# Order of work in a hybrid decoder layer: first group's routing and decoding first, then the second group's natural projections

## The chip, the cores and the metric

The kernel runs on one core of one Trainium2 chip. Its metric is the device time of one execution in microseconds (us). Three runs of the kernel before took 2902.53 to 2905.03 us, with a median of 2904.23 us. Five engines work side by side: TensorE (PE: matmuls; PEld is its loading of weights), VectorE (DVE), ScalarE (ACT), GpSimd (POOL) and SyncE (SP), the last two mostly issuing transfers.

## The reference, cut to what matters

One decoder layer over 1024 tokens of width 1024, all in float32. A normalized input goes through retention (4 heads) and differential attention (4 heads), both are projected out and added to the input; then comes a feed-forward part of 16384 single-neuron experts:

```python
h = rmsnorm(x, norm_mix_g); proj = h @ w_in              # rq rk rv rg dq dk dv
x = x + concat(silu(rg) * rmsnorm(retention(rq, rk, rv)), diff_out(dq, dk, dv)) @ w_out
xb = rmsnorm(x, norm_ffn_g)
q = (xb @ wq).reshape(t, 8, 2, 128)                      # 8 heads, two halves
s = einsum('thpd,hpkd->thpk', q, subkeys)                # 128 keys a half
s_top, i_top = top_k(s, 16)                              # of each half
c_top, c_idx = top_k(all 256 sums of two halves, 16)
e = i1 * 128 + i2; g = softmax(c_top)                    # 128 experts a token
act = gelu(einsum('thkd,td->thk', u[e], xb))
x = x + einsum('thk,thkd->td', g * act, v[e]); return rmsnorm(x, final_norm_g)
```

## The kernel before, in words

The 1024 tokens are eight tiles of 128. The first three tiles are the first group (`gs` in the code, tiles 0 to 2, "sparse"), the last five the second (`gd`, tiles 3 to 7, "dense"). Both go through `front`, a generator that emits the steps of a group: normalization and transposing (`split_t`, L197), two natural projections (`proj_n`, L176: token rows out, weights `wn`, four chunks each; up to the mark "projected"; the second one is evacuated through `dvt` tiles and written to HBM at L234 to L237), head projections (`proj_t`), retention and attention by head (up to "mixed"), a third natural projection, the output projection (L403, up to "summed"), a second normalization with transposing (L411 to L427, up to "routing"), and routing (L433 to L470): for each of 16 query blocks 24 projection matmuls (`psT`), a copy by ScalarE, the scores (`psc`, L445), and top-16 searches on VectorE; every second block also searches the sums.

All matmuls on weights take a float32 operand as two parts: a chunk of weights is loaded (`wraw`, four buffers), ScalarE makes the high part (L152, tag `uh`) and VectorE the low part (L154, `wlo`, tag `ul`), two buffers of each, and three matmuls are made of each product (L159 to L161).

The feed-forward part is done in two ways. For the first group the chosen rows of `u` and `v` are gathered: 3 tiles x 128 choices, one indirect DMA of 512 KB by GpSimd and one VectorE instruction for each row of `u` (L860, L862) and of `v` (L867, L869), 768 gathered rows in all; here a gathered row means one such step of 128 tokens. Before that, `sparse_routes` (L529) decodes the choices of each tile into indices (`decode`, L482, one-hot comparisons L505 to L514; indices at L537). For the second group all 128 x 128 experts are computed densely on TensorE (`psH`, `psHs` for inputs, `kp`, `psV` for outputs), with a gate matrix `g_d` built in between (`dense_routes`, `build_g`).

The gathered rows, the decoding tiles and several others of the early stages (among them `dvt`) share one group of five buffers, `ug`. At the end of the program `xt` and the running sum of a tile of gathered rows take the places (`sx`, `sa`) of the first group's routing results, which decoding reads.

Order is set in two ways. The order of the program text is the priority by which a planner, which works with a simulated timeline at build time, fixes the order of instructions on each engine; `weave(a, b, na, nb)` (L650) interleaves two generators at na steps to nb. The gathered rows come last in the text, so they have the lowest priority and go into VectorE's free places. They are held back by `gated` (L673): each step that passes through it adds `per` permissions, and the n-th gathered instruction is planned no sooner than the VectorE instruction that was the last one when the n-th permission was given. After the last such permission all others come free with the first dense expert (L807).

Around the change the order before is: the first group up to "summed", woven with the second group's first normalization; the second group's two natural projections (8 steps) woven 8 to 19 with the first group's second normalization and routing; then the second group from its head projections to "routing" (80 steps), woven 6 to 1 with `sparse_routes` (3 steps), at 1.5 permissions a step; then dense routing with spilled experts, gate matrices, and the dense experts.

Of the kernel before, what the change touches and what calls it, by code (L numbers as in the profile page):

```python
# [48 lines left out]
RAW = 4  # L49
UG = 5  # L50
BIGS = 4
ROUTE = 6
MIX = 3
ACTS = 1
AHEAD = 1
SPILL = 39
PACE = (8, 3)
SLOW = 4
PER = (1.5, 1.5, 0.0)
NC2 = 80  # L60
TC = {"schedule_with_timeline_sim": True}

# [36 lines left out]
def layer_kernel(ctx, tc, x, wt, wn, wo, wq, sk, ut, u, v, gmix, gffn, gfin, gsub, dlam, consts, alb, out):  # L99
# [418 lines left out]
    def gates_of(rp, late, nt, tag):  # L518

        cv = late.cv.rearrange("p t h k -> p (t h) k")  # L520
        mz = rp.tile([P, 2, nt * PH], F32, tag=tag[0], bufs=tag[1], name="mz")
        V.tensor_copy(mz[:, 0], cv[:, :, 0])
        V.tensor_sub(cv, cv, mz[:, 0, :, None].to_broadcast([P, nt * PH, K]))
        A.activation(cv, cv, AF.Exp)
        V.tensor_reduce(mz[:, 1], cv, axis=AX.X, op=ALU.add)
        V.reciprocal(mz[:, 1], mz[:, 1])
        V.tensor_mul(cv, cv, mz[:, 1, :, None].to_broadcast([P, nt * PH, K]))

    def sparse_routes(rp, late, g0, nt, *rooms):  # L529

        gates_of(rp, late, nt, rooms[0])
        for lt in range(nt):
            t = ST.index(g0 + lt)
            V.tensor_copy(gA[t].rearrange("p (h k) -> p h k", h=PH), late.cv[:, lt])
            i1, i2 = decode(rp, late, lt, *rooms)
            V.scalar_tensor_tensor(i1, i1, float(NK), i2, op0=ALU.mult, op1=ALU.add)
            V.tensor_copy(idxA[t].rearrange("p (h k) -> p h k", h=PH), i1)  # L537
            yield

    def dense_routes(rp, gp, pp, late):  # L540

        before = None
        gates_of(rp, late, ND, ("mz", 1))
        for t in range(ND):
            i1, i2 = decode(rp, late, t)
            ps = pp.tile([P, 4, P], F32, tag="B", bufs=2, name="psR")
            for c, src in enumerate((i2, i1, late.cv[:, t])):
                PE.transpose(ps[:, c], src.rearrange("p h k -> p (h k)"), ident)
            r = rp.tile([P, P // 8, 4, 8], F16, tag="rt", bufs=2, name="rt")
            by = ps.rearrange("p c (q t) -> p q c t", t=8)  # L550
            A.activation(r[:, :, 0:2], by[:, :, 0:2], AF.Copy)
            A.activation(r[:, :, 2], by[:, :, 2], AF.Copy, scale=GS)
            V.scalar_tensor_tensor(r[:, :, 3], by[:, :, 2], GS, r[:, :, 2], op0=ALU.mult, op1=ALU.subtract)
            lo = rp.tile([P, P // 8, 8], F32, tag="rl", bufs=2, name="rl")
            if ACTS:
                A.activation(lo, r[:, :, 3], AF.Copy)
            if before is not None:
                yield from build_g(gp, pp, *before)
            else:
                yield  # L560
            before = r, lo, t
        yield from build_g(gp, pp, *before)
# [84 lines left out]
    def pool(name, es=ctx, **kw):  # L647
        return es.enter_context(tc.tile_pool(name=name, bufs=1, reuse_waits="tile", **kw))

    def weave(a, b, na=1, nb=1):  # L650

        i = j = 0
        while a is not None or b is not None:
            if b is None or (a is not None and i * nb <= j * na):
                i += 1
                try:
                    yield next(a)
                except StopIteration:
                    a = None
            else:  # L660
                j += 1
                try:
                    yield next(b)
                except StopIteration:
                    b = None
# [3 lines left out]
    def last_dve():  # L669
        ins = nc.cur_bb.bb.instructions  # L670
        return next(i for i in reversed(ins) if i.engine == V.engine).name

    def gated(g, per):  # L673

        due = 0.0
        for y in g:
            due += per[y == "turned"]
            while due >= 1.0:
                gates.append(last_dve())
                due -= 1.0  # L680
            yield y

    def run(g):
        for _ in g:
            pass

    def until(g, mark):
        for y in g:
            if y == mark:
                return  # L690
            yield y

    sp = pool("sp")
# [34 lines left out]
    def spills(pf):  # L728
        for i, ei in enumerate(early):
            two = pf.tile([P, 2, 512], F32, tag="A", bufs=2, name="psHs")  # L730
            SY.dma_start(hs_d[i], experts_in(ei, lambda hf: two[:, hf]))
            yield

    with ExitStack() as es:
        pf = pool("pf", es, space=bass.MemoryType.PSUM)
        ms, md = SimpleNamespace(), SimpleNamespace()
        with ExitStack() as e2:
            fs = pool("fs", e2)
            ms.tp = ms.vp = ms.fp = ms.hp = ms.np = md.tp = fs
            md.hp, md.np, md.vp = wp, wp, lp  # L740
            ug = ("ug", UG)
            ms.big = md.big = (sp, *ug)
            lates = Routed(sp, sn, ("sx", "sa"))
            gs = front(ms, pf, cst, s0, sn, False, lates)
            gd = front(md, pf, cst, d0, dn, True, late)
            with ExitStack() as e3:
                ms.ap = pool("fa", e3)
                run(until(gs, "normed"))
                front_consts(cst, cp, wp)
                run(until(gs, "mixed"))  # L750
            run(weave(until(gs, "summed"), until(gd, "normed"), 15, 5))
            run(weave(until(gd, "projected"), gs, 8, 19))
        with ExitStack() as e2:
            fd = pool("fd", e2)
            md.tp = md.ap = md.fp = fd
            md.big = (fd, "big", BIGS)
            run(gated(weave(until(gd, "routing"), sparse_routes(sp, lates, s0, sn, ug, ug, ug), ROUTE, 1), PER[:2]))
            gh = spills(pf)
            run(weave(gd, islice(gh, 16 // SLOW), SLOW, 1))
        gp = pool("gp", es)  # L760
        run(gated(weave(dense_routes(gp, gp, pf, late), gh, *PACE), (PER[2], 0)))

# [89 lines left out]
    for t in range(NS):  # L852
# [5 lines left out]
        for k in range(HK):  # L858
            ug = sp.tile([P, D], F32, tag="ug", bufs=UG, name="ug")
# [49 lines left out]
```

## Time and profile before

| | before |
|---|---|
| runs | 2902.53 to 2905.03 us, median 2904.23 |
| profiled execution | 2900.81 us, span 2899.0 us |
| mean granted TensorE clock | 0.975 |
| PE busy | 2712.1 us (94%), 16043 matmuls |
| DVE busy | 2363.5 us (82%) |
| ACT busy | 1063.9 us (37%) |
| POOL busy | 1047.4 us (36%) |
| DMA | 741.34 MB, mean 256 GB/s |

The span runs from the first to the last instruction of the profiled execution; 1.8 us of its time lie outside. Matmuls are pipelined: one takes some 0.3 to 0.4 us in the records, while the next starts 0.14 to 0.23 us after it, so pitches are read from starts. The granted clock is the share of the full TensorE clock that was given in a stretch. A busy share over the whole span is a mean over stages with different limits; the rows below take stages apart.

### The profile page before, as it was taken

The page shows a single profiled execution, that of the slowest core. Times are in us where ns is not written, and L with a number is a line of the kernel's source. Part 1 is how long each engine was busy: PE and PEld are TensorE (multiplying, and loading weights), DVE is VectorE, ACT ScalarE, POOL GpSimd, SP SyncE. Part 2 cuts the span into 40 slices and gives each one's busy share as a digit, 9 for nine tenths or more (in the row PEclk, how much of TensorE's full clock was granted, in tenths as well). Part 3 has the DMA queues.
Part 4 walks back from the last instruction along what each step waited for, and adds up shares of the span by engine and source line. Part 5 has one row for each costly group of instructions (what it writes and reads, how often), then busy time and mean ns, then how long its engine had stood idle before and what let it go on. Part 6 is the DMA issues. An engine that isn't in the chain of part 4 may idle for free.

```text
span 2899.0 us, 43071 instructions
## 1 busy us (share of the span) xinstructions
PE 2712.1 (94%) x16043; PEld 2441.4 (84%) x16043; DVE 2363.5 (82%) x4547; ACT 1063.9 (37%) x1881; POOL 1047.4 (36%) x782
## 2 busy tenths in 40 slices
PE   7979988988889999998898998999999999999998
PEld 6868877876789999997787887899999999989987
DVE  3555899888589988985788887888889888888988
ACT  4653334544232369992222222222223222222222
POOL 0000004434310000003454443666565556655664
PEclk9989998999989999999999999999999999999999
DMA  5334236756742246668988898999999999999997
GB/s 167 105 126 146 95 113 234 242 195 236 246 150 82 87 153 236 250 257 299 313 303 285 307 326 289 347 321 344 337 333 351 325 345 341 336 343 326 341 339 259
DMA packets 292805, 741.34 MB, mean 256 GB/s; under 512 B 23401, under 2 KB 117609, under 8 KB 292594
## 3 DMA queue, kind: packets, MB, share of 16 engines
q0 software_dynamic: 111744, 404.28, 39.1%
q1 hardware_dynamic: 180850, 334.31, 33.4%
q8 instruction: 126, 2.06, 0.3%
q14 instruction: 85, 0.70, 0.1%
HBM read 670.14 MB, written 68.35 MB: 255 GB/s over the span
## 4 chain that ended last, share of the span: by engine, by line
PE 46%; DVE 14%; DMA 10%; issue 9%; POOL 3%; ACT 3%; SPq 0%; POOLq 0%; DVEq 0%; ACTq 0%
PE psH L721 6%; PE psH L722 6%; PE psH L720 6%; DMA gt<-g_d 4%; PE psV L794 4%; PE psV L795 3%; PE psV L796 3%; DMA ug<-in_u,idx 2%; PE kp L795 2%; PE kp L796 2%; PE kp L794 2%; PE psHs L720 2%; PE psHs L722 2%; DVE sa L869 2%; PE psHs L721 2%
## 5 line engine op out<-in xcount | busy, mean ns | idle before, releaser
L867 POOL DMA_INDIRECT vg<-in_v,idx x384 | 530.1, 1381 | 915.2 <-DVE ug L862 517.0
L860 POOL DMA_INDIRECT ug<-in_u,idx x384 | 511.9, 1333 | 502.7 <-DVE ug L862 335.4
L869 DVE SCALAR_TENSOR_TENSOR sa<-vg,shs,sa 128x1024 f32<-128x1024 f32 x384 | 491.9, 1281 | 40.5 <-DMA vg<-in_v,idx 36.9
L862 DVE SCALAR_TENSOR_TENSOR ug<-ug,sx 128x1024 f32<-128x1024 f32 x384 | 460.6, 1219 | 72.9 <-DMA ug<-in_u,idx 72.2
L720 PE MATMUL psH<-nh,uh 128*128 128x320 f32 x1424 | 439.6, 309 | 0.7 <-ACT uh L706 0.7
L721 PE MATMUL psH<-nl,uh 128*128 128x320 f32 x1424 | 439.7, 309 | 0.0
L722 PE MATMUL psH<-nh,ul 128*128 128x320 f32 x1424 | 438.6, 309 | 0.8 <-DVE ul L708 0.8
L794 PE MATMUL psV<-vh,wh 128*128 128x512 f32 x768 | 305.5, 399 | 29.3 <-DVE acc L830 27.5
L795 PE MATMUL psV<-vl,wh 128*128 128x512 f32 x768 | 304.4, 397 | 0.0
L796 PE MATMUL psV<-vh,wl 128*128 128x512 f32 x768 | 297.1, 397 | 0.0
L720 PEld LDWEIGHTS psH<-nh,uh 128*128 128x128 f32 x1424 | 267.4, 188 | 6.8 <-ACT uh L706 1.5
L721 PEld LDWEIGHTS psH<-nl,uh 128*128 128x128 f32 x1424 | 267.5, 188 | 5.1
L722 PEld LDWEIGHTS psH<-nh,ul 128*128 128x128 f32 x1424 | 267.2, 188 | 4.6 <-DVE ul L708 1.6
L723 ACT ACTIVATE ga<-psH 128x320 f32<-128x320 f32 x178 | 74.6, 426 | 407.5 <-PE psH L722 368.4
L706 ACT ACTIVATE uh<-uraw 128x1024 fp32r<-128x1024 f32 x128 | 135.6, 1059 | 207.1 <-PE psH L721 110.2
L720 PE MATMUL psHs<-nh,uh 128*128 128x320 f32 x624 | 197.0, 317 | 9.3 <-ACT ga L723 9.1
L154 DVE TENSOR_TENSOR wlo<-wraw,whi 128x1024 fp32r<-128x1024 f32 x104 | 126.7, 1219 | 93.0 <-ACT whi L152 90.9
L794 PEld LDWEIGHTS psV<-vh,wh 128*128 128x128 f32 x768 | 147.4, 192 | 61.9 <-DVE acc L830 30.5
L795 PE MATMUL kp<-vl,wh 128*128 128x512 f32 x512 | 198.3, 391 | 0.9 <-DVE vl L818 0.9
L152 ACT ACTIVATE whi<-wraw 128x1024 fp32r<-128x1024 f32 x104 | 110.0, 1058 | 241.6 <-PE psT L160 117.6
L794 PE MATMUL kp<-vh,wh 128*128 128x512 f32 x512 | 192.3, 391 | 5.3 <-ACT wh L810 5.3
L721 PE MATMUL psHs<-nl,uh 128*128 128x320 f32 x624 | 195.1, 313 | 0.0
(243 smaller groups left out, 6159.0 us busy)
## 6 DMA issues: line engine op xcount, KB each, us to landing
uraw<-in_ut SPq DMA_DIRECT2D x128, 512.0 KB, 6.3
vraw<-in_v SPq DMA_DIRECT2D x128, 512.0 KB, 6.8
g_d<-st SPq DMA_DIRECT2D x80, 512.0 KB, 4.9
gt<-g_d SPq DMA_DIRECT2D x32, 1280.0 KB, 18.0
wraw<-in_wt SPq DMA_DIRECT2D x32, 512.0 KB, 3.7
wraw<-in_wq SPq DMA_DIRECT2D x32, 512.0 KB, 3.7
hs_d<-ga SPq DMA_DIRECT2D x39, 320.0 KB, 2.5
gl<-hs_d SPq DMA_DIRECT2D x39, 320.0 KB, 6.8
```

What stands on the lines that cost most here:

```text
L154: V.tensor_sub(lo, raw, hi.bitcast(F32))
L706: A.activation(uh, raw, AF.Copy)
L720: PE.matmul(ps, uh[:, dc], xh[:, dc, sl], start=(dc == 0), stop=False)
L721: PE.matmul(ps, uh[:, dc], xl[:, dc, sl], start=False, stop=False)
L722: PE.matmul(ps, ul[:, dc], xh[:, dc, sl], start=False, stop=(dc == DC - 1))
L794: PE.matmul(ps, Wh[e][:, sl], Vh[e][:, so], start=start, stop=False)
L795: PE.matmul(ps, Wh[e][:, sl], Vl[e][:, so], start=False, stop=False)
L796: PE.matmul(ps, Wl[e][:, sl], Vh[e][:, so], start=False, stop=stop)
L860: G.indirect_dma_start(out=ug, out_offset=None, in_=u, in_offset=bass.IndirectOffsetOnAxis(ap=idxA[t][:, k:k + 1], axis=0))
L862: gate(V.scalar_tensor_tensor(ug, ug, 1.0, xt, op0=ALU.mult, op1=ALU.mult, accum_out=hs[:, k:k + 1]))
L867: G.indirect_dma_start(out=vg, out_offset=None, in_=v, in_offset=bass.IndirectOffsetOnAxis(ap=idxA[t][:, k:k + 1], axis=0))
L869: gate(V.scalar_tensor_tensor(ac, vg, hs[:, k:k + 1], ac, op0=ALU.mult, op1=ALU.add))
```

## The change

The change puts all of the first group's second normalization and routing ahead (`run(gs)`), then gives its decoding (`sparse_routes`) one step, and weaves the remaining two steps of decoding with the eight steps of the second group's natural projections, 4 to 1. This stage goes through `gated` with a new rate of 4.0 permissions a step (10 steps). The stage after it, from the second group's head projections on, holds `gd` alone, at 1.5 a step as before. `ROUTE`, the ratio of the former weaving, goes.

```diff
-ROUTE = 6
...
-PER = (1.5, 1.5, 0.0)
+PER = (1.5, 1.5, 0.0, 4.0)
...
             run(weave(until(gs, "summed"), until(gd, "normed"), 15, 5))
-            run(weave(until(gd, "projected"), gs, 8, 19))
+            run(gs)
+            gr = sparse_routes(sp, lates, s0, sn, ug, ug, ug)
+            run(islice(gr, 1))
+            run(gated(weave(until(gd, "projected"), gr, 4, 1), (PER[3], 0)))
         with ExitStack() as e2:
             fd = pool("fd", e2)
             md.tp = md.ap = md.fp = fd
             md.big = (fd, "big", BIGS)
-            run(gated(weave(until(gd, "routing"), sparse_routes(sp, lates, s0, sn, ug, ug, ug), ROUTE, 1), PER[:2]))
+            run(gated(until(gd, "routing"), PER[:2]))
             gh = spills(pf)
```

## Rows read from the trace of the kernel before

**Rows 1.** Stretches: limits, length, busy us of PE, PEld, DVE, ACT, POOL, clock, DMA, GB/s

```profile
273.00:401.00 128.00, 115.52 (x636) 105.49 (x635) 102.69 (x586) 41.80 (x63) 0.00 (x0) 1.00 0.32 105
401.00:460.00 59.00, 50.77 (x325) 47.64 (x325) 58.12 (x165) 22.05 (x45) 6.25 (x8) 0.97 0.37 113
460.00:600.00 140.00, 116.64 (x733) 103.53 (x732) 118.58 (x216) 65.97 (x169) 72.13 (x62) 0.90 0.77 259
600.00:795.00 195.00, 169.60 (x896) 139.76 (x894) 143.56 (x271) 75.73 (x176) 71.62 (x58) 0.94 0.66 226
795.00:811.00 16.00, 5.50 (x26) 4.30 (x26) 15.57 (x29) 7.30 (x19) 6.18 (x5) 0.68 0.73 269
1330.00:1850.00 520.00, 480.41 (x2275) 408.16 (x2274) 417.42 (x482) 118.23 (x156) 250.39 (x177) 0.96 0.88 305
1850.00:2850.00 1000.00, 1000.00 (x5627) 913.17 (x5626) 881.69 (x1061) 256.92 (x368) 614.73 (x449) 1.00 0.95 338
```

**Rows 2.** Timeline of the end: start us, us, engine, line, operation

```profile
2883.60 1.28 DVE L869 SCALAR_TENSOR_TENSOR sa<-vg,shs,sa 128x1024 f32<-128x1024 f32 x1
...
2888.42 0.39 PE L796 MATMUL psV<-vh,wl 128*128 128x512 f32 x1
```

**Rows 3.** Timeline of TensorE at routing's end, weight loads left out

```profile
393.60 0.94 PE L445 MATMUL psc<-skt,pqT 128*128 128x128 f32 x6 [1.35 <-ACT pqT L437]
...
400.06 0.94 PE L445 MATMUL psc<-skt,pqT 128*128 128x128 f32 x6 [1.35 <-ACT pqT L437]
400.75 0.39 PE L159 MATMUL psT<-hh,whi 128*128 128x320 f32 x1
```

**Rows 4.** TensorE ahead of routing: a timeline row, and a group of 246 to 273

```profile
248.60 0.39 PE L161 MATMUL psN<-whi,ml 128*128 128x512 f32 x1
...
L161 PE MATMUL psN<-whi,hl 128*128 128x512 f32 x30 | 11.9, 397 | 0.0
```

**Rows 5.** Timeline of TensorE at the second group's second normalization

```profile
793.65 0.39 PE L159 MATMUL psN<-whi,mh 128*128 128x512 f32 x1
...
794.78 0.39 PE L161 MATMUL psN<-whi,ml 128*128 128x512 f32 x1
795.32 1.29 PE L207 MATMUL psX<-ident,xn 128*128 128x128 f32 x8
805.65 1.94 PE L207 MATMUL psX<-ident,xn 128*128 128x128 f32 x8 [9.05 <-DVE xn L422]
...
810.67 0.63 PE L159 MATMUL psT<-nh,whi 128*128 128x320 f32 x1
```

**Rows 6.** Stretches, line 862 alone: VectorE's busy us; two instructions a gathered row

```profile
795.00:811.00 16.00, 6.44 (x11) 0.68 0.73 269
460.00:600.00 140.00, 65.28 (x108) 0.90 0.77 259
600.00:795.00 195.00, 69.97 (x116) 0.94 0.66 226
```

**Rows 7.** Groups of VectorE, 273 to 401: busy us, mean ns, idle before

```profile
L154 DVE TENSOR_TENSOR wlo<-wraw,whi 128x1024 fp32r<-128x1024 f32 x22 | 26.7, 1212 | 5.3 <-ACT whi L152 5.3
L452 DVE FIND_INDEX8 ti<-tv,sc 128x8 uint32<-128x128 f32 x45 | 12.2, 284 | 0.0
```

**Rows 8.** Groups of VectorE, 401 to 461: the one-hot work of decoding

```profile
L511 DVE TENSOR_TENSOR eq<-eq 128x1024 f16<-128x1024 f16 (+2 forms) x18 | 9.0, 511 | 0.1
L508 DVE TENSOR_TENSOR eq<-eq,late 128x2048 f16<-128x2048 f16 x6 | 7.3, 1222 | 0.1
L505 DVE TENSOR_TENSOR eq<-iok,c 128x2048 f16<-128x2048 f16 x6 | 7.3, 1222 | 0.0
```

**Rows 9.** Timelines of VectorE and GpSimd: decoding's indices and the first gathered row

```profile
429.66 0.22 DVE L537 CAST idx<-tmps 128x128 int32<-128x128 f32 x1
...
445.95 1.24 DVE L505 TENSOR_TENSOR eq<-iok,c 128x2048 f16<-128x2048 f16 x1
...
446.92 1.15 POOL L860 DMA_INDIRECT ug<-in_u,idx  x1 [35.19 <-DVE idx L537]
```

## The prediction

> **What bounds the kernel now.** I read the stretches of the span first, because a busy share over the whole span hides which stage waits. From 1850 to 2850 us TensorE is busy 1000.00 of 1000.00 us at a granted clock of 1.00, while VectorE has 882 of 1000 and the DMA engines 0.95 [rows 1]. Whatever else happens there, the end is set by matmuls. Before that TensorE is not full. It idles 12.5 us in 273 to 401, 8.2 us in 401 to 460, 23.4 us in 460 to 600, 25.4 us in 600 to 795, 10.5 us in 795 to 811, and 39.6 us in 1330 to 1850 (length less busy time of each row) [rows 1]. The other two streams end together: the last gathered row is added at 2883.60 us and the last matmul starts at 2888.42 us [rows 2]. So gathered rows have about 5 us to spare, and moving rows forward gains time only if it removes idle time of TensorE ahead of 1850 us.
>
> The kernel may add 124 gathered rows (83 steps at 1.5) before the dense experts; the changed one 160 (10 steps at 4.0, then 80 at 1.5). The remaining 608 instead of 644 run after it. In the last 1000 us they are fetched at 449 per 1000 us [rows 1], so 36 fewer make that stream end 36 / 0.449 = 80 us sooner, under a TensorE that is full anyway. I give this nothing.
>
> **The change, step by step.** The sum is the time at which TensorE starts the second group's first head projection (400.75 us before [rows 3]), plus what changes behind it.
>
> *The normalization ahead of routing.* Before, 30 matmuls of each of the three products, 90 in all, of the second group's natural projections lie in 246 to 273 us [rows 4], between the transposes of the first group. They now come after routing, and nothing else may take their place: weight chunks go through two buffers in program order, and the next two are routing's. Only transposes and their inputs are left. The second group has this very stage: its last output matmul is issued at 794.78, then eight transposes, a wait of 9.05 us for VectorE, and routing's first matmul at 810.67 us [rows 5]. That is 15.9 us, with 11 instructions of gathered rows for 6.4 us on VectorE in it [rows 6], which the first group will not have. So 9.5 to 15.9 us from the end of the output projection. That end is about 249 us: the first group's last output matmul is issued at 248.60 [rows 4]. Routing starts at 258.5 to 265; I take 261.
>
> *Routing alone.* One query block is 24 projection matmuls, a wait of 1.35 us for ScalarE's copy, and the scores. Where no projection chunk lies between, scores follow scores after 400.06 - 393.60 = 6.46 us [rows 3]. Sixteen blocks take 103 us. VectorE needs nearly as much: 102.7 us busy in 273 to 401 [rows 1], less 6 splits of projection chunks (22 less 16, at 1.212 us) is 95.4 us for 45 of 48 token tiles, hence 102 us for all [rows 7]. Two engines at the same limit with only two buffers between them lose a little; between 103 and 112 I take 105. Routing ends at 366 us; before, its last scores were at 400.06.
>
> *The projections alone.* 8 chunks x 30 matmuls x 0.226 us (five steps from 793.65 to 794.78 [rows 5]) = 54 us, and now all of it follows routing. Of the first chunk some fits into the last waits of routing, between nothing and a chunk (6.8 us); I take 3. TensorE comes to 417 us: 16 us later than 400.75. The ends are 9 (258.5 + 103 + 47.5 = 409 to 410) and 30 (265 + 112 + 54 = 431).
>
> *The clock after the new hole.* In 795 to 811, where the engine stood still most of the time, the granted clock was 0.68, a mix of its two levels (1.2 and 2.4 GHz) [rows 1]. I add 2 us for the first blocks at the lower level, with ends at 0 and 5.
>
> *Decoding.* The one-hot work of decoding costs 9.0 + 7.3 + 7.3 = 23.6 us of VectorE and fell into 401 to 460 [rows 8], where VectorE was busy 58 of 59 us and TensorE idled 8.2 us [rows 1]. It moves beside the projections, where VectorE otherwise has only 8 splits (10 us of 54), and is hidden. The gain is at most those 8.2 us. I take 5.
>
> *The gathered rows.* I doubt that they will lie beside the projections at all. They share five buffers with decoding and with the second projection's evacuation tiles. Before, the first row was issued at 446.92 us though the first tile's indices were written at 429.66; the last one-hot tile of decoding, which comes earlier in the program and takes such a buffer, started at 445.95 [rows 9]. If buffers go out in program order, as this looks, the rows must now wait for the evacuations at the end of the projections, about 415 us. The 40 permissions that they have by then are spent in the attention stage: there 54 + 58 rows [rows 6] went with 23.4 + 25.4 = 48.8 us of idle TensorE [rows 1], 0.44 us a row if rows were its only cause. So 36 more cost 0 to 16 us; I take 7, since attention has dependent chains of its own. VectorE's work there hardly changes: 36 x 1.21 = 44 us come, 23.6 us go, and in 460 to 600 it has 21 us free.
>
> *Dense routing, spilled and dense experts.* Same instructions, same priorities: 0. The idle time in 1330 to 1850 belongs to 177 fetched rows at most [rows 1], 0.22 us each, and the list that follows is as dense as before; 36 rows fewer are worth 0 to -8 us.
>
> Sum: 16 + 2 - 5 + 7 + 0 = **+20 us** on the profiled 2900.81 us (span 2899.0), hence 2921; the median shown is 3.4 us above the profiled run, so **2924 us**. Its own range, from the ends, is +6 to +36: 2910 to 2940.
>
> The Trainium skill, "Perfetto Trace Analysis", section "Optimization Strategy", advises to interleave regimes whose busiest engine differs. Here it speaks on both sides: the change takes apart routing (VectorE) and projections (TensorE), and wants to put projections beside gathered rows (DMA). By the second half alone the result would be the first rival's 2884 us; by the first, mine.
>
> **The rivals.**
> 1. *Faster: rows really lie beside the projections.* The routing stage has a DMA share of 0.32 [rows 1], so there is room. If the planner starts gathers as soon as indices exist and lets projection matmuls into routing's waits, TensorE reaches attention at about 402 us, with decoding (-8) and 36 to 40 rows already done. With them go 0.44 us each in attention, -16 us; so +1 - 8 - 16 = -23, say 2884 us with some loss kept. For it: VectorE was full in 401 to 460. Against it: the buffer order of [rows 9], which would also keep the projections' weight chunks behind routing's. It decides from the first gathered row issued before 400 us. Chance 0.16.
> 2. *Faster by the end: the row stream sets it.* Both streams end 5 us apart [rows 2]. If matmuls were only paced by VectorE's order, 36 rows x 1.21 us = 44 us would come off, against +20: 2880 us. Against it: TensorE has no idle time in 1850 to 2850. Chance 0.06.
> 3. *No change.* The ends meet: +9 for the start, -8 for decoding, and rows cost nothing: 2904 to 2906 us. Chance 0.14.
> 4. *The rows choke attention.* With 40 permissions at its start, rows run at the buffers' own speed instead of 1.5 a step, VectorE (118.6 of 140 us busy in 460 to 600 [rows 1]) becomes the bound there, and the start comes at its late end: 30 + 5 + 16 = +51: 2955 us. Chance 0.08.
>
> **How the numbers follow.** My forecast has 0.56, rival 4 another 0.08: slower 0.64. Rivals 1 and 2 make faster 0.22, rival 3 same 0.14. (A difference under 0.2%, 5.8 us, can't be told from none.) The range 2887 to 2943 us leaves out most of rivals 1, 2 and 4, about 0.2 in all.
>
> **What would show it.** Right: TensorE without projection matmuls from 249 to about 360 us, 30 us or more of extra idle time before 420; scores every 6.5 to 7 us; the head projections' first matmul at 410 to 430 us; no gathered row before about 410; rows ending some 70 to 90 us ahead of the last matmul; 1850 to 2850 as full as before. Wrong: projection matmuls between routing blocks, a first gathered row before 400 us, or a stage from 420 to 820 that is shorter than the 410 us of before by more than 8 us. The forecast fails if the last 1000 us shrink.

## The result, and the profile after

The changed kernel takes 2926.71 us (median; 2918.9 to 2931.94), the kernel before 2905.03 us in the same comparison. The ratio is 1.0073 with an interval of 1.0053 to 1.0093, so the change costs 21 us, between 15 and 27. One of the five runs of the kernel before took 5382.68 us; it counts in that median (2904.63 without it) but not in the ratio. The profiled execution took 2926.71 us with a span of 2924.9, 25.9 us more than the span of before; the mean granted clock is 0.975 in both, and both execute the same 16043 matmuls.

The stretches of the changed kernel, core 0, with the columns of [rows 1]. The limits follow the stages where these have moved: the hole ahead of routing, routing, projections, attention, and the last two as before.

```profile
246.00:260.00 14.00, 7.21 (x34) 5.48 (x32) 10.83 (x22) 7.86 (x20) 0.00 (x0) 0.75 0.67 245
260.00:363.00 103.00, 83.13 (x477) 77.84 (x477) 93.91 (x571) 29.39 (x46) 0.00 (x0) 0.98 0.26 86
363.00:417.00 54.00, 54.00 (x243) 44.79 (x242) 49.41 (x149) 15.45 (x20) 2.35 (x4) 1.00 0.34 108
417.00:830.00 413.00, 342.20 (x1979) 294.12 (x1978) 339.68 (x595) 174.21 (x411) 204.65 (x163) 0.92 0.77 266
...
1330.00:1850.00 520.00, 471.20 (x2235) 399.12 (x2235) 404.81 (x494) 117.97 (x156) 235.31 (x170) 0.96 0.87 302
1850.00:2850.00 1000.00, 999.73 (x5612) 911.58 (x5612) 869.56 (x1022) 260.88 (x371) 589.86 (x433) 1.00 0.93 332
```

TensorE idles 19.9 us in routing's 103, where projections lay before [rows 1, 3]; then projections alone fill it, 54.00 of 54.00 us. Before, projections and routing overlapped: from 246 us to the head projections it took 155 us with 13.1 us of TensorE idle (246 to 401), now it takes 171.5 us with 26.7 idle. The last 1000 us stand as full as they did.

TensorE's timeline of the changed kernel at the places of [rows 2 to 5]: start, us, line, operation, idle time before it and its releaser.

```profile
251.44 1.29 PE L206 MATMUL psX<-ident,xn 128*128 128x128 f32 x8 [3.56 <-DVE xn L421]
...
259.69 0.69 PE L158 MATMUL psT<-nh,whi 128*128 128x384 f32 x1
...
262.50 0.52 PE L159 MATMUL psT<-nl,whi 128*128 128x384 f32 x1
262.82 0.50 PE L160 MATMUL psT<-nh,wlo 128*128 128x384 f32 x1
...
263.70 0.33 PE L158 MATMUL psT<-nh,whi 128*128 128x384 f32 x1
263.87 0.33 PE L159 MATMUL psT<-nl,whi 128*128 128x384 f32 x1
...
267.29 0.94 PE L444 MATMUL psc<-skt,pqT 128*128 128x128 f32 x6 [1.35 <-ACT pqT L436]
273.74 0.94 PE L444 MATMUL psc<-skt,pqT 128*128 128x128 f32 x6 [1.35 <-ACT pqT L436]
...
368.77 0.83 PE L444 MATMUL psc<-skt,pqT 128*128 128x128 f32 x6
...
417.83 0.31 PE L160 MATMUL psT<-hh,wlo 128*128 128x320 f32 x1
...
828.57 1.94 PE L206 MATMUL psX<-ident,xn 128*128 128x128 f32 x8 [4.36 <-DVE xn L421]
830.34 0.64 PE L158 MATMUL psT<-nh,whi 128*128 128x320 f32 x1
...
833.10 0.36 PE L160 MATMUL psT<-nh,wlo 128*128 128x320 f32 x1
...
2914.15 0.39 PE L798 MATMUL psV<-vh,wl 128*128 128x512 f32 x1
```

Routing starts at 259.69 us, its scores follow each other every 6.45 us, the last are at 368.77, and the head projections are under way at 417.8.

Timelines of VectorE, GpSimd and SyncE of the changed kernel: decoding's indices, its last multiplication by the routing results (`late`), the first gathered row, and the last one (compare [rows 2, 9]).

```profile
397.77 0.30 DVE L536 CAST idx<-tmps 128x128 int32<-128x128 f32 x1
...
410.04 0.29 DVE L536 CAST idx<-tmps 128x128 int32<-128x128 f32 x1
...
411.92 1.29 DVE L507 TENSOR_TENSOR eq<-eq,late 128x2048 f16<-128x2048 f16 x1
...
413.24 0.33 SPq L856 DMA_DIRECT2D sx<-xn_d  x1
...
417.39 0.23 DVE L536 CAST idx<-tmps 128x128 int32<-128x128 f32 x1
...
418.48 1.01 POOL L862 DMA_INDIRECT ug<-in_u,idx  x1 [37.01 <-PE psN L160]
...
425.03 1.23 DVE L864 SCALAR_TENSOR_TENSOR ug<-ug,sx 128x1024 f32<-128x1024 f32 x1 [4.22 <-DMA ug<-in_u,idx]
...
2830.61 1.28 DVE L871 SCALAR_TENSOR_TENSOR sa<-vg,shs,sa 128x1024 f32<-128x1024 f32 x1
```

The first indices are there at 397.77, but the first row is issued at 418.48, when the projections are over, and reaches VectorE at 425.03. The tile `sx` that it is multiplied with is loaded at 413.24, right behind decoding's last multiplication by `late`, whose place it takes. The row stream ends 84 us ahead of the last matmul, where it ended 5 us ahead before.

### The profile page after: what moved, and what is told of

It reads as the page before. It is cut to its first block, busy times and chain, and to the rows that moved or that the text cites. A ratio compares the mean times of both kernels' runs of the same rounds, so it can differ in the third digit from the quotient of the medians.

```text
span 2924.9 us, 43094 instructions
## 1 busy us (share of the span) xinstructions
PE 2712.6 (93%) x16043; PEld 2437.7 (83%) x16043; DVE 2362.4 (81%) x4547; ACT 1069.8 (37%) x1885; POOL 1040.6 (36%) x782
## 4 chain that ended last, share of the span: by engine, by line
PE 36%; issue 27%; DMA 9%; DVE 8%; POOL 6%; ACT 1%; POOLq 0%; SPq 0%; DVEq 0%; ACTq 0%
POOL vg L869 5%; PE psH L719 5%; PE psH L720 5%; PE psH L721 5%; DVE ug L864 3%; PE psV L796 3%; PE psV L797 3%; PE psV L798 3%; DMA gt<-g_d 3%; DMA vg<-in_v,idx 3%; DMA ug<-in_u,idx 2%; PE kp L798 2%; PE kp L796 2%; PE kp L797 2%; PE psN L159 1%
## 5 line engine op out<-in xcount | busy, mean ns | idle before, releaser
L869 POOL DMA_INDIRECT vg<-in_v,idx x384 | 515.9, 1344 | 958.1 <-DVE sa L871 867.0
L862 POOL DMA_INDIRECT ug<-in_u,idx x384 | 519.3, 1352 | 441.6 <-DVE ug L864 302.7
L707 DVE TENSOR_TENSOR ul<-uraw,uh 128x1024 fp32r<-128x1024 f32 x128 | 156.1, 1219 | 51.8 <-ACT uh L705 50.6
L818 ACT ACTIVATE vh<-vraw 128x1024 fp32r<-128x1024 f32 x128 | 130.4, 1052 | 173.9 <-PE psV L798 118.8
```

Source lines behind the costliest of these rows:

```text
L707: V.tensor_sub(ul, raw, uh.bitcast(F32))
L862: G.indirect_dma_start(out=ug, out_offset=None, in_=u, in_offset=bass.IndirectOffsetOnAxis(ap=idxA[t][:, k:k + 1], axis=0))
L869: G.indirect_dma_start(out=vg, out_offset=None, in_=v, in_offset=bass.IndirectOffsetOnAxis(ap=idxA[t][:, k:k + 1], axis=0))
```

## The experiments

Each run's own profile gave the times at which TensorE starts a stage. "Group" is the stretch from the second group's head projections (`psT` from `hh`) to its gate matrices (`psG`): attention and dense routing together. They are taken together because dense routing's first matmul is a poor border: its first matmuls run at the lower clock after a hole, and how many do depends on where the hole lies. "Early dense experts" are the first 13 full experts (`psH`). All times are us of the profiled executions. Between kernels a start compares to some 2 us only: the changed kernel, e1, e6 and e9 have the same program ahead of routing, which starts at 259.7 to 261.9 us there. The device times of e5 to e9 are of one run each.

| | head projections | gate matrices | group | early dense experts | span |
|---|---|---|---|---|---|
| before | 400.7 | 1030.1 | 629.4 | 484.4 | 2899.0 |
| e7 before, again | 400.7 | 1030.2 | 629.5 | 490.4 | 2906.9 |
| changed | 417.5 | 1045.8 | 628.3 | 493.5 | 2924.9 |
| e1 new order, 124 rows | 420.0 | 1045.3 | 625.3 | 490.3 | 2920.5 |
| e2 old order, 160 rows | 400.8 | 1044.2 | 643.4 | 490.6 | 2923.2 |
| e3 own tiles for the evacuations | 420.1 | 1059.2 | 639.1 | 490.5 | 2935.0 |
| e4 three chunks ahead of routing | 407.5 | 1042.7 | 635.2 | 490.9 | 2923.3 |
| e5 old order, no early rows | 401.7 | 969.1 | 567.4 | 510.2 | 3058.3 |
| e6 new order, no early rows | 417.7 | 980.6 | 562.9 | 502.8 | 3061.8 |
| e8 two banks for routing | 397.0 | 1059.3 | 662.3 | 490.6 | 2935.2 |
| e9 new order, later rows | 418.0 | 1056.4 | 638.4 | 487.0 | 2931.1 |
| e10 old order, rows 1.2 / 2.35 | 401.5 | 1034.5 | 633.0 | 490.6 | 2908.9 |
| e11 old order, rows 0.9 / 3.1 | 402.3 | 1024.5 | 622.2 | 498.6 | 2908.5 |

### The order alone, and the rows alone

e1 keeps the changed order and brings the permissions back to 124.

```diff
-PER = (1.5, 1.5, 0.0, 4.0)
+PER = (1.5, 1.5, 0.0, 0.4)
```

> The changed order, with 0.4 permissions a step in place of 4.0 in the stage of the natural projections, so that 124 gathered rows (4 + 120) come before the dense experts, as in the kernel before, in place of 160. Theory A, the order costs: the head projections start at 417 us again (before 400.75) and the time stays within 5 us of the changed kernel, 2920 to 2930 us. Theory B, the 36 more rows cost (crowded attention stage, and the dense experts' first 500 us, which lost 10 us): the stage from the first head projection to dense routing, 413 us with the change, falls to about 400, the stretch from the first to the last matmul of the dense experts goes from 1571 back to about 1561, and the time to 2900 to 2910 us.

2926.43 us, ratio 1.0071 (1.0050 to 1.0092): the order alone costs what the whole change costs. All of it lies ahead of 420 us. The group gains 4.1 us (629.4 to 625.3): decoding has left it, and its first row reaches VectorE at 427.80 us instead of 456.98.

e2 keeps the order of before and adds the 36 permissions.

```diff
+            gates += [last_dve()] * 36
             run(gated(weave(until(gd, "routing"), sparse_routes(sp, lates, s0, sn, ug, ug, ug), ROUTE, 1), PER[:2]))
```

> The order of before, with 36 permissions given at once ahead of the head projections, so that 160 gathered rows come before the dense experts. Theory A, the order costs: head projections at 401 us as before, time within 5 us of before, 2900 to 2910 us. Theory B, the rows cost: the stage from the head projections to dense routing grows from 410 us by 5 to 16 us, the dense experts from 1561 to about 1571 us, time 2916 to 2930 us.

2924.57 us, ratio 1.0059 (1.0038 to 1.0079): the rows alone cost almost as much. The group grows by 14.0 us, 0.39 us for each of the 36 rows. The stretch of attention in e2, and what TensorE waits for in it (engine and line, releaser: us in total, times, longest):

```profile
401.00:829.00 428.00, 343.91 (x1976) 296.00 (x1974) 378.86 (x728) 174.69 (x411) 208.62 (x168) 0.91 0.75 259
```

```profile
PE psA L367 <- DVE e L360: 18.9, 10, 6.8
PE ret L275 <- DVE am L273: 14.9, 4, 5.7
PE psT L159 <- ACT pt L298: 13.8, 4, 6.6
```

VectorE is busy 379 of 428 us, and single waits for the attention weights that it combines (`e`) last up to 6.8 us. VectorE and TensorE of e2 at the end of the longest one:

```profile
651.96 1.23 DVE L863 SCALAR_TENSOR_TENSOR ug<-ug,sx 128x1024 f32<-128x1024 f32 x1 [0.85 <-DMA ug<-in_u,idx]
...
655.44 1.21 DVE L863 SCALAR_TENSOR_TENSOR ug<-ug,sx 128x1024 f32<-128x1024 f32 x1
...
656.58 1.15 DVE L360 SCALAR_TENSOR_TENSOR e<-e,rz,e 128x896 f32<-128x896 f32 x1
...
657.87 1.51 PE L367 MATMUL psA<-ident,e 128*128 128x128 f32 x6 [6.84 <-DVE e L360]
```

Rows stand ahead of `e` in VectorE's order, and for the first of these VectorE even idles 0.85 us until the transfer lands. The two halves of the change do not add: at the gate matrices the order alone is 15.2 us late, the rows alone 14.1, and both together 15.7.

### No early rows, in either order

e5 (the kernel before) and, likewise, e6 (the changed one, four rates) set the rates to zero; all 768 rows come in the dense experts.

```diff
-PER = (1.5, 1.5, 0.0)
+PER = (0.0, 0.0, 0.0)
```

> The order of before with no permissions ahead of the dense experts: no gathered rows beside attention, all 768 after it, decoding still in the attention stage. What I read is that stage, from the first head projection to dense routing (410 us with 124 rows, 428 with 160). If rows are the cause of TensorE's idle time there at 0.44 us each, it takes 410 - 124 x 0.44 = 355 us. If attention's own chains are, it stays above 395 us. The whole time grows either way, since 768 rows at about 0.43 a us take some 1790 us from 1330 on: 3070 to 3150 us.

> The changed order with no permissions ahead of the dense experts. Against the run before it this shows what decoding costs in the attention stage without rows. If VectorE's 24 us of one-hot work held TensorE up there, the stage is 5 to 20 us shorter than with decoding in it; if decoding only ever costs by its collision with rows, the two stages agree within 4 us. The head projections start at 417 us as with the change.

The times, 3060.34 and 3064.59 us, are set by the row stream, which ends nearly 200 us behind the last matmul; what counts is the attention stage. For e5 the stretch of attention, the one behind the last matmul, and TensorE's longest waits in attention:

```profile
402.00:751.00 349.00, 320.11 (x1975) 278.71 (x1974) 205.15 (x444) 172.40 (x409) 10.06 (x13) 0.98 0.26 85
...
2856.00:3050.00 194.00, 0.00 (x0) 0.00 (x0) 149.22 (x122) 2.89 (x6) 144.96 (x109) 0.51 0.88 306
```

```profile
PE psX L207 <- DVE xn L422: 4.4, 1, 4.4
PE psN L160 <- DVE wlo L154: 4.4, 2, 4.1
...
PE psA L367 <- DVE e L360: 2.4, 5, 0.6
```

Without rows the waits for `e` shrink from 18.9 us in e2 to 2.4, none over 0.6: it is the rows that made them long. The group takes 567.4 us instead of 629.4: 124 rows cost TensorE 62 us, 0.50 each. In the new order 160 rows cost 65.4 us (628.3 less 562.9), 0.41 each, and 124 rows 62.4. Decoding's departure is worth 4.5 us without rows (567.4 to 562.9), at the border of the two outcomes that were expected.

### The kernel before, profiled again

> The kernel before, unchanged, profiled a second time. The five changed orders so far all show the stretch from the first matmul of the dense experts to the fourteenth full expert at 490 to 494 us, the profile of before 484 us. If that profile was a quick one, this one shows 488 to 494 us there; if the order before is really better placed there, 482 to 487 us again.

2908.68 us, span 2906.9. Up to the early dense experts every start of a stage agrees with the first profile within 0.1 us; these then take 490.4 instead of 484.4 us. So the first profiled execution was a quick one there, and 6 of the 25.9 us between the profiles are not the change's.

### Can the rows lie beside the projections?

e3 takes the evacuations of the second projection out of the buffers that they share with the rows.

```diff
-            dvt = big([P, 512], "dvt")
+            dvt = wp.tile([P, 512], F32, tag="ga", bufs=2, name="dvt")
```

> The changed kernel, with the evacuation tiles of the second natural projection taken from another pair of buffers, not from the five that gathered rows use. If buffers go out in program order and these tiles held the rows back, the first gathered row is issued at 380 to 400 us, not at 418, and 15 to 30 rows lie beside the projections. What they are worth: by the first rival 0.44 us for each row taken out of the attention stage, 7 to 13 us less than the changed kernel (2914 to 2920 us); by my forecast, in which rows cost attention little, within 6 us of it. If the first row stays at 418 us, the buffer order is not what held it.

2942.39 us, ratio 1.0123 (1.0099 to 1.0147). The first row was issued at 413.78 us, not at 380 to 400. Timelines of VectorE, GpSimd and SyncE of e3:

```profile
400.38 0.27 DVE L536 CAST idx<-tmps 128x128 int32<-128x128 f32 x1
...
412.63 0.28 DVE L536 CAST idx<-tmps 128x128 int32<-128x128 f32 x1
412.76 1.28 DVE L504 TENSOR_TENSOR eq<-iok,c 128x2048 f16<-128x2048 f16 x1
413.78 6.25 POOL L862 DMA_INDIRECT ug<-in_u,idx  x1 [29.73 <-DVE idx L536]
...
414.50 1.28 DVE L507 TENSOR_TENSOR eq<-eq,late 128x2048 f16<-128x2048 f16 x1
...
415.81 0.33 SPq L856 DMA_DIRECT2D sx<-xn_d  x1
...
425.46 1.22 DVE L864 SCALAR_TENSOR_TENSOR ug<-ug,sx 128x1024 f32<-128x1024 f32 x1 [5.88 <-DMA ug<-in_u,idx]
```

The row stands right behind decoding's last one-hot tile, as in [rows 9]. So the evacuations held the issue only for the last 5 us (7 us, if one allows for e3's stages starting 2.6 us later); before that it was decoding, itself late because VectorE is nearly full beside the projections (49.41 of 54 us). On VectorE the edit moved nothing: the first row is there at 425.46 us, in the changed kernel at 425.03. A second lock explains that. The load of `sx` waits for decoding's last multiplication by `late`: it is issued at 415.81 us here and at 413.24 in the changed kernel, each within 0.1 us of that multiplication's end. What fills VectorE beside the projections, its groups of the changed kernel in 363 to 417 show (busy us, mean ns, idle before):

```profile
L153 DVE TENSOR_TENSOR wlo<-wraw,whi 128x1024 fp32r<-128x1024 f32 x8 | 10.0, 1250 | 0.0
...
L504 DVE TENSOR_TENSOR eq<-iok,c 128x2048 f16<-128x2048 f16 x6 | 7.6, 1271 | 0.0
L507 DVE TENSOR_TENSOR eq<-eq,late 128x2048 f16<-128x2048 f16 x6 | 7.6, 1270 | 0.0
```

In this program no row can be worked on before decoding has read `late` for the last time, for all three tiles, whichever buffers are free. What rows beside the projections would be worth, e3 does not tell, since there were none. Its group is 10.8 us longer than the changed kernel's, in part by the edit itself: the evacuation tiles now share `ga` with `qT`, and TensorE waits 8.3 us in all for `qT` where it waited 2.6. The rest was not settled.

### Filling the holes again

e4 puts three of the eight chunks back beside the first group's second normalization, in the hole ahead of routing, and spreads the 40 permissions over the seven steps that remain.

```diff
-PER = (1.5, 1.5, 0.0, 4.0)
+PER = (1.5, 1.5, 0.0, 5.72)
...
+            run(weave(until(gs, "routing"), islice(gd, 3), 1, 1))
             run(gs)
```

> The changed kernel, but the first three of the eight chunks of the natural projections lie beside the first group's second normalization, as they did before; 160 rows early, as with the change. By my sum of the front the hole ahead of routing closes (20 us of matmuls go in, routing starts at about 273 instead of 260), routing alone takes 103 us again, five chunks follow (34 us): head projections at 408 to 412 us, 6 to 9 us sooner than with the change, and the time 6 to 9 us less, 2917 to 2921 us. If the start does not move, the hole was not what it cost.

2927.0 us, ratio 1.0069 (1.0045 to 1.0093). The head projections start at 407.5, 10 us sooner, about as expected, but the time did not move, a miss: the group takes 635.2 us, 6.9 more. Decoding's last indices are now written at 438 us, inside attention, instead of 417.4, which may be why. The rest is within what two runs differ by.

e8 shortens routing's blocks instead: its projections alternate between two accumulation banks.

```diff
-            for a, b, ps in proj_t(wq[hp], nx, "TR"):
+            for a, b, ps in proj_t(wq[hp], nx, "TR" if len(halves) > 1 else "TR"[hp % 2]):
```

> The changed kernel, with the projections of the first group's routing in two PSUM banks in turn, so that TensorE need not wait 1.35 us for ScalarE's copy in each block. If VectorE is at the same limit as TensorE while routing runs alone, as my sum has it (102 against 103 us), the sixteen blocks still take 98 to 103 us and the head projections start 1 to 5 us sooner. If the wait was the only limit, the blocks come every 5 us, and the head projections start 20 us sooner.

2936.95 us. TensorE and VectorE of e8 at two blocks' scores, the last index of routing, and the first head projection; then its attention stage:

```profile
304.93 0.83 PE L444 MATMUL psc<-skt,pqT 128*128 128x128 f32 x6
309.79 0.83 PE L444 MATMUL psc<-skt,pqT 128*128 128x128 f32 x6
...
373.11 0.26 DVE L456 CAST late<-ti 128x96 f16<-128x96 uint32 x1
...
397.02 0.30 PE L158 MATMUL psT<-hh,whi 128*128 128x320 f32 x1
```

```profile
397.00:843.00 446.00, 353.22 (x1978) 301.68 (x1977) 357.57 (x631) 175.36 (x414) 202.97 (x164) 0.90 0.72 250
```

A block takes 4.86 us on TensorE instead of 6.45, and the head projections start 20.5 us sooner: the 20 expected if the wait were the only limit, not the 1 to 5 of the sum. But VectorE's last index of routing comes at 373.11 instead of 375.38 us and decoding's last indices at 415.4 instead of 417.4: VectorE was at the same limit (busy 56.97 of 57 us from 340 to 397), and what TensorE gained it gave back, with 34 us more in the group. Of these, 20.5 are the earlier start; the other 13.5 are a loss that was not taken apart. The Trainium skill, "Perfetto Trace Analysis", section "Optimization Strategy", says that the same gap repeated on the engine that should be saturated can point to too few buffers. The trace agrees about the gap, which one more bank closed; it was worth nothing, since VectorE was at its limit there too.

### When the rows start

e9 keeps the new order and 160 rows, but gives the first permissions only in attention.

```diff
-PER = (1.5, 1.5, 0.0, 4.0)
+PER = (1.5, 1.5, 0.0, 0.0)
...
-            run(gated(until(gd, "routing"), PER[:2]))
+            head = until(gd, "routing")
+            run(islice(head, 8))
+            gates += [last_dve()] * 52
+            run(gated(head, PER[:2]))
```

> The changed order, but no permissions until eight steps of the head projections have passed (as late into the attention stage as decoding let the rows start before), then 52 at once and 1.5 a step: 160 rows again. With 160 rows the attention stage took 428 us in the order before (decoding in it, rows from 56 us into it) and 413 us in the changed one (decoding ahead of it, rows from 8 us into it). If decoding's collision with the rows made the 15 us, the stage stays at 410 to 416 us here. If it was the later start, which crowds the rows, it goes to 422 to 430 us.

2932.86 us. A permission holds back VectorE's part of a row, not its gather (e6, which permits none, still issues its first gather at 418.61 us), so the first row on VectorE counts, here in e9 and then in e2:

```profile
450.82 1.22 DVE L867 SCALAR_TENSOR_TENSOR ug<-ug,sx 128x1024 f32<-128x1024 f32 x1
```

```profile
457.00 1.26 DVE L863 SCALAR_TENSOR_TENSOR ug<-ug,sx 128x1024 f32<-128x1024 f32 x1
```

The group of e9 takes 638.4. From e2 (643.4) to e9 decoding leaves the group and rows start 6 us sooner: 5.0 us, the third measure of decoding. From e9 to the changed kernel (628.3) the rows start 26 us sooner, and the group is 10.1 us shorter. By this an earlier start pays for most of what the 36 rows cost, 14.0 us in the old order against 3.0 in the new one (625.3 to 628.3). It is argued from single profiles, and e9 also hands out 52 permissions at once.

### A better place for the rows in the old order

e5 showed that rows cost most in attention's first part (up to the step `mixed` 296 us with 85 rows against 239 without; from there to dense routing 114 against 111). e10 and e11 therefore keep the kernel before and move permissions behind it, 1.2 and 2.35 a step, or 0.9 and 3.1.

```diff
-            run(gated(weave(until(gd, "routing"), sparse_routes(sp, lates, s0, sn, ug, ug, ug), ROUTE, 1), PER[:2]))
+            run(gated(weave(until(gd, "mixed"), sparse_routes(sp, lates, s0, sn, ug, ug, ug), ROUTE, 1), (1.2, 1.2)))
+            run(gated(until(gd, "routing"), (2.35, 2.35)))
```

> The order of before and 124 rows before the dense experts, as before, but 1.2 permissions a step up to the end of attention (59 steps, 70 rows) and 2.35 after it (23 steps, 54 rows), in place of 1.5 throughout. Without rows the part up to the end of attention took 239 us and with them 296, the part behind it (natural projections) 111 and 114: 0.66 us a row against 0.08. So 17 rows fewer in the first part give back 11 us and cost 1 to 3 in the second: 8 to 10 us faster than before, ratio 0.996 to 0.998. If rows cost the same wherever they lie in the stage, ratio 1.000.

> As the run before it, with 0.9 permissions a step up to the end of attention (53 rows) and 3.1 after it (71 rows). The first part gives back 35 x 0.66 = 23 us. But 71 rows in some 114 us are 0.62 a us, more than the 0.45 at which rows are fetched elsewhere, so some 20 fall into dense routing, where VectorE is full, and cost 1.2 us each there. Ratio 0.995 to 1.000; if rows cost the same everywhere, 1.000.

2905.78 us, ratio 0.9991 (0.9982 to 1.0000), and 2908.18 us, 1.0005 (0.9996 to 1.0014): no gain that can be told, a miss. In e10's profile the group did not shrink (633.0 us, where 8 to 10 us less were expected). In e11 it is 7.2 us shorter, and the early dense experts take 498.6 instead of 490.4 us: given back at once. No version here beats the kernel before.

## Why the prediction was right

The forecast was slower, 2924 us for 2926.71, and its mechanism is what the traces show: TensorE is full from 1850 us on, so only idle time ahead of it counts, and the change adds some.

- *Start of routing*: 261 forecast, 259.69 measured. *Routing alone*: 105 us with 16 blocks of 6.46; the last scores came at 368.77 instead of 366. *Projections*: TensorE is full with them, and 28 of their 240 matmuls fit in ahead of the last scores, some 6 us instead of 3, which makes up for the later end. *Head projections*: 417 forecast, 417.5 measured: +16.8 us. The Trainium skill, "Perfetto Trace Analysis", section "Optimization Strategy", advises to interleave regimes with different busiest engines; taking routing and projections apart cost these 16.8 us, so for that half the trace agrees.
- *The clock*: the granted clock is 0.75 in the hole. Routing's first matmuls follow each other after 0.32 us up to 263.1 us and after 0.17 us from there on (its two levels), so the first block takes 7.6 us from its first matmul to its scores, the next ones 5.8. That is the 2 us of the forecast; but they were added behind 417, and the measured start already holds them, so start and clock together were put 1 us too high.
- *Decoding*: −5 forecast; −4.1 (e1), −4.5 (e6 against e5) and −5.0 (e9 against e2) measured, of which only e6 against e5 is free of the rows' start. The size was right. The reason that VectorE "otherwise has only 8 splits" beside the projections left out that decoding (some 33 us with its small instructions) and routing's tail (9 us) would fill that stage: decoding was hidden, but nothing else could be.
- *The rows*: first row at "about 415", measured 418.48, none beside the projections. The reason given, the buffers of the evacuations, explains only the last 5 to 7 us of the issue (e3); ahead of that decoding held them, by its own buffers and by the place of `sx`, a lock that the prediction left out. The cost, 7 us within 0 to 16, was over twice the 3.0 measured (and the times of e1 and of the changed kernel do not differ at all). That the same rows cost 14.0 in the old order, and 124 rows 0.50 us each, shows that 0.44 us a row was near the mark; what the sum did not have is that rows may start earlier here, which seems to pay for part of it.
- *The rest*: 0 to −8 forecast. From the gate matrices to the end the changed kernel takes 1879.1 us, the kernel before 1868.9, and 1876.7 when profiled again. No gain, and no loss that two profiles can tell. Dense routing alone seems 4 us shorter after (its first matmul to the gate matrices: 215.4 for 219.4), but that is the border between the stages: before, 7.0 us of its matmuls run at the lower clock (one every 0.267 instead of 0.147 us), after the change 2.8, which is worth 1.9 us; and transposes and a wait, 1.7 us, lie on the other side of its first matmul now.

The sum, by the steps: 16.8 - 4.1 + 3.0 = 15.7 us at the gate matrices, and 2.4 us from there on against e7; the timed difference is 21 us, with 15.4 to 27 as its interval. That the forecast of +20 lies so close is partly luck: the rows were put 4 us too high, and 2.4 us behind the gate matrices and some 3 us that no step shows make up for it. Each part alone was not foreseen either: the sum makes the order alone +13 and the rows alone +7, and 15.2 and 14.1 were measured at the gate matrices. The range of +6 to +36 is also narrower than what the ends of its terms add up to, -7 to +51, and the prediction gives no working for it. Rival 1 (rows beside the projections) fell by its own sign, the first row; rival 2 by the row stream, which now ends 84 us early while the time did not fall; rival 3 needed +9 for the start; rival 4 by the group, which did not grow. One sign did not come: TensorE's idle time from 246 us to the head projections grew by 13.6 us, not by "30 us or more". With the same matmuls, a start 16 us later left no room for 30, so the sign was at odds with the prediction's own sum.

Two things stay open. Runs with 160 rows reach the gate matrices between 1042.7 and 1059.3 us and their head projections start between 397 and 420, with no common order (e8 is first in the one and last in the other); what in each written order decides it was not taken apart. So the late start is where the change loses, but e4 takes back 10 us of it and e8 all of it, and neither is faster than the changed kernel. Against e2, with as many rows, e8 has the head projections 3.8 us sooner and decoding over 45 us sooner, and its group is 19 us longer, so a re-planned order can hide or feign a term of some us. And what rows beside the projections would bring if decoding lay elsewhere was not tried.

## What to carry to other kernels

Find the stretch in which the bounding engine is full: a side stream that ends earlier under it is worth nothing, and the 36 rows brought forward here gained nothing at the end. Two parts of a change that cost 15.2 and 14.1 us alone cost 15.7 together, so each part has to be run with and without the other before either is blamed. And before work is moved beside a stage, look at what the same change already puts there: VectorE's 44 free us beside the projections were filled by decoding and the tail of routing, and a row's work had to wait for the end of decoding anyway, because it uses the place of what decoding reads.

## What the runs showed of the hardware

A gathered row holds VectorE for one operation of 1.22 us (of `u`) or 1.28 us (of `v`), and TensorE felt 0.50 us a row in attention, although VectorE was busy only 336 of 410 us there. Of VectorE's 74 idle us, 31.0 were spent waiting for a row whose transfer had not landed (20 waits, the longest 4.5 us), with later work behind it: a side stream can hold up the bounding engine long before the engine that carries it is full. And TensorE made 20.5 us faster in routing (e8) left the kernel slower than the change did, by 34 us more in the next stage.
